# x1 transposed part by part without its norm, the norm applied one stage later, and the later modulation's tiles loaded by GpSimd's queue

## The chip, the cores and the metric

The kernel runs on one core of one Trainium2 chip. The metric is the device time of one execution in microseconds (us), and the median over the executions of one kernel is what two kernels are compared by. Inside a core, TensorE (PE in the profile) multiplies matrices, VectorE (DVE) and ScalarE (ACT) work on tiles elementwise, GpSimd (POOL) and SyncE (SP) mostly issue DMA transfers here. Each engine works through its own instructions in the order in which the program wrote them, and waits at an instruction until the data that it needs are there.

## The reference

One block of a hybrid network for 256 tokens of width 2048, in float32:

```python
cs = silu(c)
mod = cs @ ada_w + ada_b
sh1, sc1, g1, sh2, sc2, g2 = split(mod, 6)
h = rmsnorm(x, norm1_w) * (1 + sc1) + sh1
...                      # h @ w_in, gated delta net -> o_a, sparse attention -> o_b
y = sigmoid(m_a) * (o_a @ w_branch_gdn) + sigmoid(m_b) * (o_b @ w_branch_nsa)
x = x + g1 * (y @ w_out)
h2 = rmsnorm(x, norm2_w) * (1 + sc2) + sh2
x = x + g2 * peer(h2, peer_wq, ...)
return rmsnorm(x, final_norm_w)
```

The change is at the line `x = x + g1 * (y @ w_out)`, called x1 below, at the line `h2 = ...`, and at the loading of the part of `ada_w` from which g1, sh2 and sc2 are made.

## The kernel before

Weights come from HBM as float32. To multiply in a faster number format without losing accuracy, each weight piece of 128x512 is cut in two: ScalarE casts it (`whi<-raw`), VectorE takes the rest (`wlo<-raw,whi`), and TensorE does three products, hi*hi, lo*hi and hi*lo. A class `Stream` does this for all weights in order: SyncE's queue loads 512 KB tiles into 4 buffers `raw`, `advance` cuts as many pieces ahead as there are buffers (5 in the first stream, 4 in the second), and `get` hands out the next piece.

The stages that matter here, in order of time: the projections of h with the gated delta net as side work, attention, the two branch products (`wn`), then `y @ w_out` in four column blocks j = 0 to 3 of 512 columns (`wo`), then h2 and its first product with `peer_wq` (`wq`). Tokens stand in two blocks of 128, tb = 0 and 1.

**Side work.** Tasks written as Python generators are put in a list `bg`; between the groups of main matmuls a planner with its own rough cost model of every engine and of two DMA queues decides which task's next step is written into the program. So an edit that changes a modelled cost also changes the order in which later side work stands. One such side work is `ada_late`: 192 tiles `adas` of 128x512 (256 KB) with the columns of `ada_w` for g1, sh2 and sc2 are loaded into two buffers, and VectorE multiplies each with `crow` and sums it (`SCALAR_TENSOR_TENSOR adas<-adas,crow`). The load of a tile is written right behind the multiplication that frees its buffer. The same function runs again much later for g2, into tiles that the trace calls `ht`.

**wo, before.** For each block j, `x1_part` multiplies the sums in PSUM with g1 (`x<-ps,g1b`), adds x (`x<-x,xr`), lets ScalarE square the result and sum it into `ss1`, and stores it (`x1d`). In block 3 the last four row tiles are done for tb 0 first and then for tb 1, each followed by its part and by `x1_norm`, which makes r1 = 1/rms for the 128 tokens, and from it `dg`, a diagonal matrix.

**h2, before.** `h2_pairs` multiplies x1 with `dg` on TensorE: this transposes x1 and applies the norm at once, into PSUM. Three pairs stand ahead of the loop over the 16 row tiles k, the others in it. In the loop ScalarE makes the hi part from PSUM with scale and bias, VectorE makes the float32 value (`h32b`) from PSUM and subtracts, and TensorE does 12 matmuls of 256 columns with the wq piece of the row tile before.

All operations are recorded at one helper line, L294, so tiles tell them apart.

Of the kernel before, what the change touches and what calls it, by code (L numbers as in the profile page):

```python
# [160 lines left out]
def flat(ap, off, *dims):  # L161
    return bass.AP(tensor=ap.tensor, offset=ap.offset + off, ap=[list(x) for x in dims])
# [16 lines left out]
NO1 = 4  # L179
TKT = 2  # L180
GEND = 20.0
NPAIR = 3
ZPACE = 5.0
NGT = 3
NSET = 2
# [225 lines left out]
def _build(nc, tc, A, out, stacks, dump, at, stop_at):  # L411
# [300 lines left out]
        act(out, in_, AF.Sqrt, bias=epst, scale=scale)  # L712
        V.reciprocal(out, out)

    def ada_late(parts, crow, acol, row, room):

        raws = []
        n = 64 * len(parts)

        def load():  # L720
            m = len(raws)
            r = room(m)
            SP.dma_start(r, flat(A["ada_t"], (64 * (parts[m // 64] - 2) + m % 64) * 128 * 512, (512, 128), (1, 512)))
            raws.append(r)

        for _ in range(2):
            load()
        yield
        for i, part in enumerate(parts):
            for m in range(64):  # L730
                r = raws[64 * i + m]
                q = m % 4
                V.scalar_tensor_tensor(r, r, 1.0, crow(q), op0=OP.mult, op1=OP.mult,
                                       accum_out=acol[:, m // 4, q:q + 1])
                if len(raws) < n:
                    load()
                yield
            col = mcol[:, part, :]
            V.tensor_reduce(col, acol, axis=AX.X, op=OP.add)
            V.tensor_tensor(col, col, adabT[:, 16 * part:16 * part + 16], OP.add)  # L740
            if part == SC2:
                V.scalar_tensor_tensor(col, col, 1.0, n2T, op0=OP.add, op1=OP.mult)
            if part in (G1, G2):
                yield bg.now() + 4.0
                p = ps()
                PE.transpose(p[:16, 0:128], col, ident)
                S.copy(row, p[:16, 0:128])
                G.dma_start(flat(modr, D if part == G2 else 0, (128, 16), (1, 128)), row)
            done.add(part)
            yield  # L750

    ada_gen = ada_late((G1, SH2, SC2), lambda q: crow[:, 512 * q:512 * q + 512], sbp.tile([128, 16, 4], F32, name="acol"),
                       sbp.tile([16, 128], F32, name="adarow"),
                       lambda m: sbp.tile([128, 512], F32, name="adas", bufs=2))

    def ada_until(*parts):

# [277 lines left out]
    def kv_rot(a, o, dst, free):  # L1035

        rts = []
        for tb in range(2):
            r = rp.tile([128, 2, 128], F32, name="kv_t", bufs=3)
            S.copy(r, a[tb][:, o:o + 256].rearrange("p (g d) -> p g d", g=2))  # L1040
            rts.append(r)
        banks.give(free)
        yield from wait_for("rope")
        yield
        for tb in range(2):
            rope(rts[tb], rts[tb], tb, 2)
# [242 lines left out]
    def vcvs_task(a):  # L1289
        vt = []  # L1290
        for tb in range(2):
            r = rp.tile([128, 2, 128], F32, name="kv_t", bufs=3)
# [326 lines left out]

    st_1 = stack()  # L1620
    xp = pool(st_1, "xp", side=RIGHT)
    x1 = xp.tile([128, 2, D], F32, name="x1")
# [4 lines left out]
    dg = xp.tile([128, 2, 128], F32, name="dg")  # L1627

    def x1_part(tb, j, c, a, xr):
        w = WO[j][1]  # L1630
        V.tensor_tensor(x1[:, tb, c], a[:, :w], g1b[:, c], OP.mult)
        V.tensor_tensor(x1[:, tb, c], x1[:, tb, c], xr[:, tb, :w], OP.add)
        act(ps()[:, :w], x1[:, tb, c], AF.Square, accum_out=ss1[:, tb, j:j + 1])
        G.dma_start(x1d[tb, :, c], x1[:, tb, c])

    def x1_norm(tb):
        r = r1[:, tb:tb + 1]
        V.tensor_reduce(r, ss1[:, tb, :], axis=AX.X, op=OP.add)
        rsqrt(r, r, 1.0 / D)
        V.tensor_scalar(dg[:, tb, :], ident, r, None, op0=OP.mult)  # L1640

    def xr_load(j):
        o, w = WO[j]
        xr = xp.tile([128, 2, 512], F32, name="xr", bufs=2)
        G.dma_start(xr[:, :, :w], A["x"][:, :, o:o + w].rearrange("b p d -> p b d"))
        return xr

    xrs = [xr_load(0)]
    for j, (o, w) in enumerate(WO):
        c = slice(o, o + w)  # L1650
        xr = xrs[j]
        if j + 1 < len(WO):
            xrs.append(xr_load(j + 1))
        if j < len(WO) - 1:
            po = dense_all(f"wo{j}", oT(yh), oT(yl), 16, w) if j else po0
            for tb in range(2):
                x1_part(tb, j, c, po[tb], xr)
        else:
            act(r1, ss1[:, :, 0], AF.Sqrt)
            po = acc2()  # L1660
            dense(po, oT(yh), oT(yl), w, range(16 - NLAST), 0, 15)

            last = [stream.get() for _ in range(NLAST)]
            for tb in range(2):
                for i, (h, l) in enumerate(last):
                    k = 16 - NLAST + i
                    PE.matmul(po[tb][:, :w], oT(yh)(k, tb), h[:, :w], start=False, stop=False)
                    PE.matmul(po[tb][:, :w], oT(yh)(k, tb), l[:, :w], start=False, stop=False)
                    PE.matmul(po[tb][:, :w], oT(yl)(k, tb), h[:, :w], start=False, stop=k == 15)
                x1_part(tb, j, c, po[tb], xr)  # L1670
                x1_norm(tb)
        banks.give(2)
    ada_until(SH2, SC2)
    st_y.close()
    st_a.close()
    stream.close()
    dump("x1", x1)
    at("x1")


# [16 lines left out]
    def h2_pairs(k2s):  # L1697

        new = [ps() for _ in k2s]
        for tb in range(2):  # L1700
            for k2, p in zip(k2s, new):
                for i in range(2):
                    k = 2 * k2 + i
                    PE.matmul(p[:, i * 256 + tb * 128:i * 256 + tb * 128 + 128], x1[:, tb, k * 128:(k + 1) * 128],
                              dg[:, tb, :], start=True, stop=True)
        return new


    pairs = h2_pairs(range(NPAIR))
    q4 = [ps() for _ in range(4)]  # L1710
    for k in range(17):
        if k == 0:
            stream.advance(0)
        if k < 16:
            pk = pairs[k // 2][:, k % 2 * 256:k % 2 * 256 + 256]
            hi, lo, _ = h2_of(k)
            h32 = xp.tile([128, T], F32, name="h32b", bufs=2)
            act(hi, pk, AF.Identity, bias=mcol[:, 3, k:k + 1], scale=mcol[:, 4, k:k + 1])
            V.tensor_scalar(h32, pk, mcol[:, 4, k:k + 1], mcol[:, 3, k:k + 1], op0=OP.mult, op1=OP.add)
            V.tensor_tensor(lo, h32, hi, OP.subtract)  # L1720
            if k % 2 == 0 and len(pairs) < 8:
                pairs += h2_pairs([len(pairs)])
        if k:
            h, l = stream.get()
            hi, lo, _ = h2_of(k - 1)
            for ct in range(4):
                w, wl_ = h[:, ct * 128:(ct + 1) * 128], l[:, ct * 128:(ct + 1) * 128]
# [214 lines left out]
    def g2_task():  # L1942
# [4 lines left out]
        start = bg.now()  # L1947
        for m, v in enumerate(ada_late((G2,), lambda q: crow[q // 2][:, q % 2 * 512:q % 2 * 512 + 512],
                                       small[:, 0:64].rearrange("p (n q) -> p n q", q=4), small[0:16, 128:256],
                                       lambda m: room[:, m % 2 * 512:m % 2 * 512 + 512])):  # L1950
# [131 lines left out]
```

## Time and profile before

| | us |
|---|---|
| median of 3 executions | 2616.61 (2616.02 to 2620.22) |
| profiled execution, its time | 2617.43 |
| its span in the trace | 2615.3 |
| TensorE busy in the span | 2551.7 |
| VectorE busy | 1870.9 |
| ScalarE busy | 1416.9 |
| GpSimd busy | 520.5 |

The span is the time from the first to the last instruction in the trace; 2.1 us of the execution's time lie around it. TensorE is busy in 98% of the span, so the 64 us in which it is idle are spread over few places, and an edit tells in the time by the idle time and the work that it adds to TensorE or takes from it.

### The profile page before, as it was taken

To read this page: it belongs to the slowest core of one execution; us is meant where nothing else is said; L and a number is where in the kernel's file an instruction comes from. 1 tells how busy PE (TensorE), PEld (TensorE's weight loads), DVE (VectorE), ACT (ScalarE), POOL (GpSimd) and SP (SyncE) were. 2 spreads that over 40 slices of the span, in tenths; PEclk is the share of its full clock that TensorE was granted. 3 is DMA by queue.
4 is the path that set the end of the run, shared out by engine and by line. 5 is a ranking of instruction groups with operands and counts; after the bars stand their busy time and mean duration, and the time that the engine had idled before them with its cause. 6 is when DMAs were issued, how large, how long until landed. Compare 5 with 4: busy or idle time off the path is not lost.

```text
span 2615.3 us, 42819 instructions
## 1 busy us (share of the span) xinstructions
PE 2551.7 (98%) x14746; PEld 2121.7 (81%) x14746; DVE 1870.9 (72%) x4089; ACT 1416.9 (54%) x2907; POOL 520.5 (20%) x467
## 2 busy tenths in 40 slices
PE   7999999999999999999999999999999999999998
PEld 5777777687877877999998888888778888888886
DVE  5667777777778776889885555555588887766666
ACT  4445756556555444555555555555555555655555
POOL 0001000000000000016666666662011112000000
PEclk9999999999999999999999999999999999999999
DMA  8997866777676887456667776776698888555554
GB/s 326 333 334 267 278 222 221 236 238 268 209 252 227 293 291 265 173 181 183 178 186 186 186 189 186 189 186 199 215 308 293 289 289 292 190 189 186 190 187 153
DMA packets 229658, 605.65 MB, mean 232 GB/s; under 512 B 60032, under 2 KB 60496, under 8 KB 228800
## 3 DMA queue, kind: packets, MB, share of 16 engines
q1 hardware_dynamic: 168192, 537.29, 59.1%
q0 software_dynamic: 49728, 41.50, 9.1%
q10 hardware_dynamic: 11520, 24.12, 2.4%
q8 instruction: 116, 1.90, 0.3%
q14 instruction: 102, 0.84, 0.1%
HBM read 572.76 MB, written 30.04 MB: 230 GB/s over the span
## 4 chain that ended last, share of the span: by engine, by line
PE 84%; DVE 6%; DMA 4%; ACT 3%; issue 2%; ACTq 0%; SPq 0%; DVEq 0%; POOLq 0%
PE ps L294 84%; DVE wlo L294 2%; DMA adas<-ada_t 1%; DMA raw<-w_in 1%; ACT whi L294 1%; DMA ht<-ada_t 1%; DVE adas L294 1%; ACT L294 1%; DVE cv L294 0%; DMA big<-x 0%; DVE A L294 0%; ACT gsq L294 0%; ACT o L294 0%; DVE x L294 0%; DMA mix<-partd 0%
## 5 line engine op out<-in xcount | busy, mean ns | idle before, releaser
L294 DVE TENSOR_TENSOR wlo<-raw,whi 128x512 fp32r<-128x512 f32 (+2 forms) x1632 | 1097.8, 685 | 508.8 <-ACT whi L294 449.6
L294 ACT CAST whi<-raw 128x512 fp32r<-128x512 f32 (+2 forms) x1632 | 996.1, 617 | 756.6 <-PE ps L294 571.7
L294 PE MATMUL ps<-ht,whi 128*128 128x256 f32 (+1 forms) x3152 | 817.7, 335 | 0.8 <-DVE ht L294 0.8
L294 PE MATMUL ps<-ht,wlo 128*128 128x256 f32 x2304 | 648.6, 281 | 0.3
L294 PEld LDWEIGHTS ps<-ht,whi 128*128 128x128 f32 x3152 | 533.6, 188 | 68.7 <-DVE ht L294 1.0
L294 PE MATMUL ps<-whi,ht 128*128 128x512 f32 (+2 forms) x1536 | 519.0, 401 | 11.2 <-ACT whi L294 7.6
L1860 POOL DMA_INDIRECT gated<-gate,place x256 | 415.2, 1622 | 287.0 <-DMA gated<-gate,place 172.9
L294 PEld LDWEIGHTS ps<-ht,wlo 128*128 128x128 f32 x2304 | 434.2, 188 | 1.0 <-DVE wlo L294 0.7
L294 PE MATMUL ps<-wlo,wh 128*128 128x512 f32 x1024 | 406.4, 397 | 3.0 <-DVE wlo L294 3.0
L294 PE MATMUL ps<-whi,wl 128*128 128x512 f32 x1024 | 406.3, 397 | 0.0
L294 PE MATMUL ps<-whi,wh 128*128 128x512 f32 x1024 | 403.1, 394 | 2.0 <-ACT wh L294 2.0
L294 PEld LDWEIGHTS ps<-whi,ht 128*128 128x128 f32 x1536 | 289.8, 190 | 86.5 <-issue 10.7
L294 PE MATMUL ps<-wlo,ht 128*128 128x512 f32 (+2 forms) x768 | 301.1, 392 | 3.1 <-DVE wlo L294 3.0
L294 PEld LDWEIGHTS ps<-wlo,wh 128*128 128x128 f32 x1024 | 192.6, 188 | 51.8 <-DVE wlo L294 4.1
L294 PEld LDWEIGHTS ps<-whi,wh 128*128 128x128 f32 x1024 | 192.6, 188 | 50.2 <-ACT wh L294 2.3
L294 PEld LDWEIGHTS ps<-whi,wl 128*128 128x128 f32 x1024 | 192.6, 188 | 44.8 <-DVE wl L294 0.2
L294 ACT CAST wh<-A 128x256 fp32r<-128x256 f32 x256 | 103.9, 407 | 134.9 <-PE ps L294 128.7
L294 PEld LDWEIGHTS ps<-wlo,ht 128*128 128x128 f32 x768 | 146.5, 191 | 32.3 <-DVE wlo L294 7.7
L294 DVE SCALAR_TENSOR_TENSOR adas<-adas,crow 128x512 f32<-128x512 f32 x192 | 131.5, 685 | 40.0 <-DMA adas<-ada_t 39.5
L294 DVE TENSOR_TENSOR wl<-A,wh 128x256 fp32r<-128x256 f32 x256 | 108.7, 425 | 47.4 <-ACT wh L294 46.6
L294 POOL DMA_DIRECT2D gates<-gated x128 | 68.6, 540 | 358.5 <-DVE A L294 346.3
L294 ACT COPY aj<-ps 128x256 f32<-128x256 f32 x91 | 33.9, 373 | 78.9 <-PE ps L294 74.6
(322 smaller groups left out, 2198.6 us busy)
## 6 DMA issues: line engine op xcount, KB each, us to landing
raw<-u SPq DMA_DIRECT2D x256, 512.0 KB
raw<-v SPq DMA_DIRECT2D x256, 512.0 KB
raw<-w_in SPq DMA_DIRECT2D x170, 512.0 KB
adas<-ada_t SPq DMA_DIRECT2D x192, 256.0 KB
raw<-ada_w SPq DMA_DIRECT2D x64, 512.0 KB
gated<-zero ACTq DMA_DIRECT2D x64, 256.0 KB
raw<-wn SPq DMA_DIRECT2D x32, 512.0 KB
raw<-wo SPq DMA_DIRECT2D x32, 512.0 KB
```

The source lines that it names most:

```text
L294: r = f(*args, **kw)
L1860: nc.gpsimd.indirect_dma_start(gated[tb].rearrange("i j (t o) -> (i j t) o", o=1), bass.IndirectOffsetOnAxis(ap=place[:, tb, n:n + 1], axi ...
```

## The change

Four things change.

1. x1 is no longer kept. `x1_part` writes the sum into the tile `xr` that held x, and `x1_turn` transposes it on TensorE with the identity, into PSUM, from where ScalarE copies it to `x1T`. For blocks 0 to 2 the square and the transpose are side work (`x1_task`); ahead of block 3 the program waits, in writing, until all their steps are written. In block 3 they stand right behind each part.
2. The norm: instead of `dg`, `x1_norm` spreads r1 over all partitions by a matmul (`ps<-ccom,r`) and a copy to `r1b`.
3. The h2 loop: VectorE makes `h32b` = x1T * scale * r1b, ScalarE makes hi from `h32b` plus the bias, and VectorE makes lo from `h32b`, the bias and hi.
4. The tiles `adas` are loaded by GpSimd's queue; the loads for g2 stay with SyncE's. `kv_t` has 4 buffers for 3.

```diff
-    def ada_late(parts, crow, acol, row, room):
+    def ada_late(parts, crow, acol, row, room, queue):
...
-            SP.dma_start(r, flat(A["ada_t"], (64 * (parts[m // 64] - 2) + m % 64) * 128 * 512, (512, 128), (1, 512)))
+            queue.dma_start(r, flat(A["ada_t"], (64 * (parts[m // 64] - 2) + m % 64) * 128 * 512, (512, 128), (1, 512)))
...
-                       lambda m: sbp.tile([128, 512], F32, name="adas", bufs=2))
+                       lambda m: sbp.tile([128, 512], F32, name="adas", bufs=2), G)
...
     def x1_part(tb, j, c, a, xr):
-        w = WO[j][1]
-        V.tensor_tensor(x1[:, tb, c], a[:, :w], g1b[:, c], OP.mult)
-        V.tensor_tensor(x1[:, tb, c], x1[:, tb, c], xr[:, tb, :w], OP.add)
-        act(ps()[:, :w], x1[:, tb, c], AF.Square, accum_out=ss1[:, tb, j:j + 1])
-        G.dma_start(x1d[tb, :, c], x1[:, tb, c])
+        x = xr[:, tb]
+        V.tensor_tensor(a, a, g1b[:, c], OP.mult)
+        V.tensor_tensor(x, x, a, OP.add)
+        G.dma_start(x1d[tb, :, c], x)
+
+    def x1_square(tb, j, xr):
+        act(ps(), xr[:, tb], AF.Square, accum_out=ss1[:, tb, j:j + 1])
+
+    def x1_turn(tb, j, xr):
+        p = ps()
+        for i in range(4):
+            PE.transpose(p[:, i * 128:(i + 1) * 128], xr[:, tb, i * 128:(i + 1) * 128], ident)
+        S.copy(x1T[:, 4 * j:4 * j + 4, tb * 128:(tb + 1) * 128], p.rearrange("p (k t) -> p k t", k=4))
+
+    def x1_task(j, xr):
+
+        yield times.ready[xr.tensor.name] + LAG
+        for tb in range(2):
+            x1_square(tb, j, xr)
+            yield
+            x1_turn(tb, j, xr)
+            yield
+        x1_done.add(j)
 
     def x1_norm(tb):
         r = r1[:, tb:tb + 1]
         V.tensor_reduce(r, ss1[:, tb, :], axis=AX.X, op=OP.add)
         rsqrt(r, r, 1.0 / D)
-        V.tensor_scalar(dg[:, tb, :], ident, r, None, op0=OP.mult)
+        p = ps()
+        PE.matmul(p[:, 0:128], r.to_broadcast([128, 128]), ident, start=True, stop=True)
+        S.copy(r1b[:, tb, :], p[:, 0:128])
...
+            bg.add(x1_task(j, xr))
         else:
+            bg.until(lambda: len(x1_done) == j)
...
                 x1_part(tb, j, c, po[tb], xr)
+                x1_square(tb, j, xr)
+                x1_turn(tb, j, xr)
                 x1_norm(tb)
...
-            h32 = xp.tile([128, T], F32, name="h32b", bufs=2)
-            act(hi, pk, AF.Identity, bias=mcol[:, 3, k:k + 1], scale=mcol[:, 4, k:k + 1])
-            V.tensor_scalar(h32, pk, mcol[:, 4, k:k + 1], mcol[:, 3, k:k + 1], op0=OP.mult, op1=OP.add)
-            V.tensor_tensor(lo, h32, hi, OP.subtract)
-            if k % 2 == 0 and len(pairs) < 8:
-                pairs += h2_pairs([len(pairs)])
+            h32 = xp.tile([128, T], F32, name="h32b", bufs=3)
+            V.scalar_tensor_tensor(h32, x1T[:, k, :], mcol[:, 4, k:k + 1], r1b.rearrange("p b t -> p (b t)"),
+                                   op0=OP.mult, op1=OP.mult)
+            act(hi, h32, AF.Identity, bias=mcol[:, 3, k:k + 1])
+            V.scalar_tensor_tensor(lo, h32, mcol[:, 3, k:k + 1], hi, op0=OP.add, op1=OP.subtract)
```

On TensorE, at the end of block 3, the matmuls of tb 0, of tb 1 and the first of the h2 loop (`ps<-ht,...`) stood together, with `dg` matmuls ahead of the loop:

```order
L294 MATMUL ps<-wlo,yh 128x512
L294 MATMUL ps<-whi,yl 128x512
L294 MATMUL ps<-dg,x_10524 128x128 x16
L294 MATMUL ps<-ht,whi 128x256 x2
L294 MATMUL ps<-ht,wlo 128x256
```

Now, between the last matmul of tb 0 and the first of tb 1 (`ccom,xr` are the transposes, `ccom,r` is the matmul that spreads r1):

```order
L293 MATMUL ps<-whi,yl 128x512
L293 MATMUL ps<-ccom,xr 128x128 x4
L293 MATMUL ps<-ccom,r_10543 128x128
L293 MATMUL ps<-whi,yh 128x512
L293 MATMUL ps<-wlo,yh 128x512
```

The transposes of tb 0 and the matmul with its r1 stand ahead of tb 1's last 12 matmuls; the same two rows stand again between tb 1 and the h2 loop. At the boundary of blocks 2 and 3 eight transposes stand in one row, `MATMUL ps<-ccom,xr 128x128 x8`.

On VectorE, from tb 1's norm into the h2 loop, before:

```order
L294 TENSOR_REDUCE r_10528<-ss_10527 128x1
L294 RECIPROCAL r_10528<-r_10528 128x1
L294 TENSOR_SCALAR dg<-ccom,r_10528 128x128
L294 TENSOR_TENSOR wlo<-raw,whi 128x512 x4
L294 TENSOR_SCALAR h32b<-ps,mcol 128x256
L294 TENSOR_TENSOR ht<-h32b,ht 128x256
```

Now on ScalarE at the same place (`ht<-h32b` makes hi):

```order
L293 ACTIVATE r_10543<-r_10543,epst 128x1
L293 COPY r1b<-ps 128x128
L293 CAST whi<-raw 128x512 x4
L293 ACTIVATE ht<-h32b,mcol 128x256 x3
L293 CAST whi<-raw 128x512
L293 ACTIVATE ht<-h32b,mcol 128x256
```

What moved is what hi hangs on: before it was made from PSUM beside `h32b`, now it is made from `h32b`. On both engines the row tiles follow each other as before, from the fourth on with one weight piece between two of them.

On GpSimd's queue, from attention's end through block 1 of wo, there is now (sa, sb, g1b and xr are loads of the mix, of g1 and of x):

```order
L293 DMA adas<-ada_t 128x512 x8
L293 DMA sa<-mixd 128x1024
L293 DMA sb<-mixd 128x1024
L293 DMA adas<-ada_t 128x512 x20
L293 DMA g1b<-modr 128x2048
L293 DMA xr<-x 128x2x512 x2
L293 DMA x1d<-xr 128x512 x2
L293 DMA xr<-x 128x2x512
L293 DMA adas<-ada_t 128x512 x9
```

Before, the `adas` rows stood on SyncE's queue, one after nearly every weight load. In the stages of the projections and attention the side work of all engines stands in another order than before; from the end of the h2 loop on, the order is the same.

## Rows read from the trace of the kernel before

**Rows 1.** The page: the span, and each engine's busy time.

```profile
span 2615.3 us, 42819 instructions
PE 2551.7 (98%) x14746; PEld 2121.7 (81%) x14746; DVE 1870.9 (72%) x4089; ACT 1416.9 (54%) x2907; POOL 520.5 (20%) x467
```

**Rows 2.** Window: length; busy time of PE, PEld, DVE, ACT, POOL; granted clock; DMA.

```profile
212.00:612.00 400.00, 381.32 (x2785) 295.15 (x2783) 297.72 (x837) 248.21 (x587) 4.91 (x14) 0.98 0.73 246
```

**Rows 3.** The critical chain: start, duration, what (two DMA pieces).

```profile
591.20 5.29 DMA mix<-partd
...
954.34 7.83 DMA adas<-ada_t
```

**Rows 4.** Waits of TensorE, 212 to 612 us, then 840 to 1045: sum, times, longest.

```profile
PE ps L294 <- DVE wlo L294: 3.0, 9, 0.7
...
PE ps L294 <- DVE wlo L294: 3.5, 5, 1.3
```

**Rows 5.** The tile adas: what VectorE waited for before it (us, times).

```profile
  DMA adas<-ada_t: 39.5, 24
```

**Rows 6.** Timeline from tb 0's last sums to the h2 loop.

```profile
1042.21 0.69 DVE L294 TENSOR_TENSOR x<-ps,g1b 128x512 f32<-128x512 f32 x1 [2.85 <-PE ps L294]
...
1043.66 0.60 ACT L294 ACTIVATE ps<-x 128x512 f32<-128x512 f32 x1 [5.03 <-DVE x L294]
...
1044.93 0.16 DVE L294 RECIPROCAL r<-r 128x1 f32<-128x1 f32 x1 [0.36 <-ACT r L294]
...
1045.47 1.60 PE L294 MATMUL ps<-dg,x 128*128 128x128 f32 x12 [0.50 <-DVE dg L294]
...
1047.93 2.16 ACT L294 CAST whi<-raw 128x512 fp32r<-128x512 f32 x4
...
1050.85 0.36 PE L294 MATMUL ps<-ht,whi 128*128 128x256 f32 x1
...
1052.03 0.39 PE L294 MATMUL ps<-ht,whi 128*128 128x256 f32 x1 [0.82 <-DVE ht L294]
```

**Rows 7.** Groups by form over the whole span: busy, mean ns, idle before.

```profile
L294 ACT CAST whi<-raw 128x512 fp32r<-128x512 f32 x1600 | 982.5, 621 | 738.7 <-PE ps L294 562.6 <-DMA raw<-w_in 65.1 <-ACT whi L294 39.7
...
L294 ACT COPY PT<-ps 128x512 f32<-128x512 f32 x16 | 9.3, 590 | 2.9 <-PE ps L294 2.3
...
L294 ACT ACTIVATE ht<-xnT,mcol 128x256 fp32r<-128x256 f32 x16 | 8.9, 594 | 1.2 <-DVE mcol L294 1.2
...
L294 ACT CAST whi<-raw 128x256 fp32r<-128x256 f32 x16 | 6.3, 409 | 4.8 <-PE ps L294 4.7
...
L294 DVE TENSOR_TENSOR wlo<-raw,whi 128x512 fp32r<-128x512 f32 x1600 | 1083.4, 690 | 498.0 <-ACT whi L294 439.2 <-PE ps L294 24.9 <-issue 3.0
...
L294 DVE SCALAR_TENSOR_TENSOR oal<-ps,gnw,oah 128x256 fp32r<-128x256 f32 x8 | 3.8, 480 | 1.1 <-ACT oah L294 1.1
```

**Rows 8.** The tile h32b: durations in ns (min/median/max), first and last start.

```profile
L294 DVE TENSOR_SCALAR h32b<-ps,mcol x16: 536/539/544, 1051.0 to 1075.9; 128x256 f32<-128x256 f32 x16
```

**Rows 9.** Timeline of TensorE: the matmul after the loop's 192nd, and four transposes.

```profile
952.68 0.60 PE L294 MATMUL ps<-ccom,sb 128*128 128x128 f32 x4
953.04 0.48 PE L294 MATMUL ps<-whi,yh 128*128 128x512 f32 x1
...
1078.40 0.40 PE L294 MATMUL ps<-ht,whi 128*128 128x256 f32 x2
```

**Rows 10.** Timeline around the boundary of blocks 2 and 3.

```profile
1026.76 2.69 ACT L294 CAST whi<-raw 128x512 fp32r<-128x512 f32 x5
...
1027.41 0.50 PE L294 MATMUL ps<-whi,yh 128*128 128x512 f32 x1 [1.22 <-ACT whi L294]
```

**Rows 11.** Windows as in rows 2: ahead of a lower clock, in it, and behind wo.

```profile
406.60:410.00 3.40, 1.43 (x8) 0.88 (x7) 3.31 (x8) 2.73 (x9) 0.00 (x0) 1.00 0.65 213
410.10:413.40 3.30, 3.14 (x9) 2.57 (x10) 1.21 (x4) 2.83 (x7) 0.00 (x0) 0.50 0.84 305
...
1045.00:1048.40 3.40, 1.60 (x12) 1.42 (x12) 2.15 (x7) 1.40 (x4) 0.54 (x1) 1.00 0.28 108
```

More of the change, by code (lines that the diff above doesn't have):

```diff
@@ L181 @@
 GEND = 20.0
-NPAIR = 3
 ZPACE = 5.0
@@ L1038, in kv_rot @@
         for tb in range(2):
-            r = rp.tile([128, 2, 128], F32, name="kv_t", bufs=3)
+            r = rp.tile([128, 2, 128], F32, name="kv_t", bufs=4)
             S.copy(r, a[tb][:, o:o + 256].rearrange("p (g d) -> p g d", g=2))
@@ L1291, in vcvs_task @@
         for tb in range(2):
-            r = rp.tile([128, 2, 128], F32, name="kv_t", bufs=3)
+            r = rp.tile([128, 2, 128], F32, name="kv_t", bufs=4)
             S.copy(r, a[tb][:, 0:256].rearrange("p (g d) -> p g d", g=2))
@@ L1621, in _build @@
     xp = pool(st_1, "xp", side=RIGHT)
-    x1 = xp.tile([128, 2, D], F32, name="x1")
+    x1T = xp.tile([128, KT, T], F32, name="x1T")
     g1b = xp.tile([128, D], F32, name="g1b")
@@ L1626, in _build @@
     r1 = xp.tile([128, 2], F32, name="r1")
-    dg = xp.tile([128, 2, 128], F32, name="dg")
+    r1b = xp.tile([128, 2, 128], F32, name="r1b")
+    x1_done = set()
     def x1_part(tb, j, c, a, xr):
-        w = WO[j][1]
-        V.tensor_tensor(x1[:, tb, c], a[:, :w], g1b[:, c], OP.mult)
-        V.tensor_tensor(x1[:, tb, c], x1[:, tb, c], xr[:, tb, :w], OP.add)
-        act(ps()[:, :w], x1[:, tb, c], AF.Square, accum_out=ss1[:, tb, j:j + 1])
-        G.dma_start(x1d[tb, :, c], x1[:, tb, c])
+        x = xr[:, tb]
[17 more added lines that the diff above has]
+        x1_done.add(j)
     def x1_norm(tb):
@@ L1639, in x1_norm @@
         rsqrt(r, r, 1.0 / D)
-        V.tensor_scalar(dg[:, tb, :], ident, r, None, op0=OP.mult)
+        p = ps()
+        PE.matmul(p[:, 0:128], r.to_broadcast([128, 128]), ident, start=True, stop=True)
+        S.copy(r1b[:, tb, :], p[:, 0:128])
     def xr_load(j):
         o, w = WO[j]
-        xr = xp.tile([128, 2, 512], F32, name="xr", bufs=2)
+        xr = xp.tile([128, 2, 512], F32, name="xr", bufs=3)
         G.dma_start(xr[:, :, :w], A["x"][:, :, o:o + w].rearrange("b p d -> p b d"))
@@ L1676, in _build @@
     stream.close()
-    dump("x1", x1)
     at("x1")
@@ L1695, in h2_of @@
         return h2[k // 2][:, k % 2, 0], h2[k // 2][:, k % 2, 1], h2[k // 2][:, k % 2].rearrange("p n t -> p (n t)")
[L1697 to L1709, printed above, removed]
     q4 = [ps() for _ in range(4)]
@@ L1714, in _build @@
         if k < 16:
-            pk = pairs[k // 2][:, k % 2 * 256:k % 2 * 256 + 256]
             hi, lo, _ = h2_of(k)
-            h32 = xp.tile([128, T], F32, name="h32b", bufs=2)
-            act(hi, pk, AF.Identity, bias=mcol[:, 3, k:k + 1], scale=mcol[:, 4, k:k + 1])
-            V.tensor_scalar(h32, pk, mcol[:, 4, k:k + 1], mcol[:, 3, k:k + 1], op0=OP.mult, op1=OP.add)
-            V.tensor_tensor(lo, h32, hi, OP.subtract)
-            if k % 2 == 0 and len(pairs) < 8:
-                pairs += h2_pairs([len(pairs)])
+            h32 = xp.tile([128, T], F32, name="h32b", bufs=3)
[3 more added lines that the diff above has]
+            V.scalar_tensor_tensor(lo, h32, mcol[:, 3, k:k + 1], hi, op0=OP.add, op1=OP.subtract)
         if k:
@@ L1949, in g2_task @@
                                        small[:, 0:64].rearrange("p (n q) -> p n q", q=4), small[0:16, 128:256],
-                                       lambda m: room[:, m % 2 * 512:m % 2 * 512 + 512])):
+                                       lambda m: room[:, m % 2 * 512:m % 2 * 512 + 512], SP)):
             yield -max(start + G2PACE * m, bg.now() + 2.0, v or 0.0)
```

## The prediction

> **What bounds the kernel now.** I read the page first: TensorE is busy in 2551.7 of 2615.3 us [rows 1]. So an edit can gain only where TensorE idles or does work that can go, and it loses wherever TensorE newly waits. Next the windows, for the places of the idle time: in the stretch of the projections it is 400 - 381.3 = 18.7 us [rows 2], and that is the largest. Then the chain and the waits, for what the loads of `adas` cost. The chain holds a load of 7.83 us from issue to use [rows 3], and VectorE waits for such loads 39.5 us in 24 places [rows 5]. But VectorE's wait reaches TensorE only after the weight pieces cut ahead have been used up: TensorE waited for `wlo` 3.0 us in the first stretch and 3.5 us in the second [rows 4]. Last the timeline from the end of wo into the h2 loop, where the arithmetic changes.
>
> There TensorE does not wait at all between the two token blocks. Its last matmul ends at 1045.47 - 0.50 = 1044.97, and tb 0's chain of norm runs from 1042.21 beside tb 1's 12 matmuls [rows 6]. The first matmul of the h2 loop starts at 1050.85, it pauses once for 0.82, and the loop's 192nd is done where the next one starts, at 1078.40 [rows 6, 9]: 33.4 us from the end of wo. Row tiles follow each other on VectorE every (1075.9 - 1051.0) / 15 = 1.66 us [rows 8].
>
> **The change, part by part.**
>
> *Transposes of blocks 0 and 1.* Four groups of four. A group keeps the next matmul back by 953.04 - 952.68 = 0.36 us [rows 9], so 4 x 0.36 = +1.4. They are side work in a stage that TensorE bounds. The squares and the 0.59 us copies [rows 7] go to ScalarE between casts, where it has room; I cost them at nothing there.
>
> *Boundary of blocks 2 and 3.* Eight transposes stand ahead of block 3's first matmul, and TensorE takes instructions in order. Multiply and add take 1043.66 - 1042.21 = 1.45 us for one token block [rows 6], two need 2.9. The first can start some 0.7 before block 2 ends, since tb 1's last three matmuls follow tb 0's. So tb 1's transposes are done 2.9 - 0.7 + 0.4 = 2.6 us after the end. Today TensorE goes on at once, then runs out of pieces and waits 1.22, because the squares and a table load on ScalarE hold the casts back until 1026.76 [rows 10]; starting 2.6 later, it should not run out. Net +1.4; the bounds are 0.8 (the transposes alone) and 2.6.
>
> *tb 0 against tb 1 in block 3.* Transposes and the matmul with r1 of tb 0 now stand ahead of tb 1's 12 matmuls, and these wait behind them. Today r1 is there at 1044.93 + 0.16 = 1045.09 [rows 6]. Now a copy of 0.59 [rows 7] stands between square and root on ScalarE, some of it in a gap, so about 1045.5; with the matmul (two records of 1.60 / 12 = 0.13 us [rows 6]) tb 1 starts at about 1045.8 instead of 1042.2. That is +3.6, and the price is sure within half a microsecond, since the rows are the same operations.
>
> *From tb 1 into the loop.* Counted from the end of wo: multiply to reciprocal 1045.09 - 1042.21 = 2.9, the copy 0.45, the r1 matmul and its handoff 0.4, the copy to `r1b` 0.3, four casts 2.16 [rows 6] beginning just before that copy ends, and the last `wlo` (0.69 [rows 7]) behind them: the first `h32b` starts 7.0 us after the end of wo. Today these casts lie beside the dg matmuls.
>
> *The loop.* In front of a row tile's hi now stands its own `h32b`, and on VectorE lo waits for that hi. From the fourth tile on, one cast stands behind hi on ScalarE and one `wlo` behind lo on VectorE, ahead of the next `h32b`. So a tile goes round: `h32b`, hi, cast, `wlo`. The trace has no such `h32b`; nearest is the 128x256 operation with one scalar per partition, 0.48. hi lies between a bare cast of that size, 0.41, and the activation with two scalars, 0.59; I take 0.50. Cast 0.62, `wlo` 0.69 [rows 7]. End to end 2.29. ScalarE begins an instruction 0.11 before the end of the one before (four casts take 2.16, not 2.48 [rows 6, 7]); with the same on both engines and three handoffs of 0.03, 2.17. Bounds 2.07 and 2.29. The first three tiles have no cast between them: 0.48 + 0.50 + 0.48 = 1.46. The last `h32b` starts at 7.0 + 2 x 1.46 + 13 x 2.17 = 38.1; hi, lo and the last matmuls add 2.5: 40.6 us after the end of wo for 33.4. That is +7.2 for both steps, though the loop loses its dg matmuls. By its own work TensorE would need 1.4 us a tile: 27.55 us from 1050.85 to 1078.40 [rows 6, 9], less the pause of 0.82, less 32 dg records at 0.13 (half of them stand in the loop, by the order), over 192 is 0.117, times 12.
>
> *The clock.* Where TensorE was busy in 1.43 of 3.4 us, the next stretch was granted 0.50, the 1.2 GHz level; behind wo, with 1.60 busy, it stayed at 1.00 [rows 11]. The new waits of 3 and 8 us hold about 0.8 us of TensorE's work each, so I expect a fall at each. A stretch at half speed costs at most 1.7 us of work, and nothing where TensorE idles. I take +2, from 0 to 5.
>
> *Loads of adas by GpSimd's queue.* They no longer stand between weight loads on SyncE, each of which waits for a buffer. 512 KB by GpSimd's queue took 5.29 us, 256 KB by SyncE's 7.83 [rows 3]. Upper bound of the gain: all of TensorE's waits for `wlo` in the two stretches, 6.5 [rows 4]. From the other side: 8 of these loads now stand behind loads of sa and sb that wait for VectorE and TensorE, and VectorE's sum, with every `wlo` behind it, waits for them; that could cost as much again as it saves. I take -4, from -6.5 to +4. GpSimd's issues cost nothing: it is busy in 520 of 2615 us [rows 1], and before the h2 stage hardly at all [rows 2].
>
> A page speaks against this step: the Trainium skill, "SBUF — State Buffer", "SBUF: two separate sides", says that while VectorE runs a copy in its two-port mode, GpSimd cannot write the descriptors of its transfers, and they stand still. Transfers by GpSimd's queue beside a busy VectorE took 5.29 us here [rows 3], which does not show it, and most of VectorE's work there is the two-input `wlo`, not copies. By the rule the term would be a loss and not -4; it is the fourth case below.
>
> *The side work's order.* In the projections every engine's order is new. I see no sign of a direction; 0, with 6 to each side, a third of that stretch's idle 18.7 [rows 2].
>
> **Sum.** 1.4 + 1.4 + 3.6 + 7.2 + 2 - 4 = +11.6 against the profiled execution's 2617.4, which makes 2629.0. The median of the runs is 0.8 lower than that execution, so 2628.2.
>
> **The rivals.**
>
> *No change:* hi is ahead, and the loop runs at TensorE's pace. Then tiles take 1.4 and not 2.17, the loop ends at about 8 + 16 x 1.4 = 30.4 instead of 40.6, and the sum is +1.4: 2618. For it speaks that three row tiles stand ahead of the first cast, and that four pieces are cut; against it, that the round through both engines is written into both orders. It becomes "no change" once a tile takes under 1.69 us, where 13 tiles give back 6.3 and the sum is 5.2.
>
> *Faster:* the new order of side work removes the projections' idle time. The price is at most 18.7, plus what the clock gives back: half-speed stretches as the one of rows 11 cost up to 1.7 each. With three quarters of the idle and two such stretches, -17.4: 2611. It decides once the projections give back 16.8, so that +11.6 becomes less than -5.2. Against it: most of that idle is waits for the delta net's own chain, only 3.0 of it for `wlo` [rows 4].
>
> *Much slower:* GpSimd's queue holds the adas loads up, and VectorE waits more than 39.5 us. If each of the 24 late loads waits for one more VectorE operation of 0.69, VectorE waits 16.6 more; the waits reached TensorE with 6.5 of 39.5 [rows 4, 5], so -4 turns into about +3, and with the loads behind sa and sb into +4: 2636.
>
> **How the numbers follow.** A measurement of this kernel tells about 0.2%, 5.2 us, from no change. I give the forecast 0.70, no change 0.12, faster 0.10, much slower 0.08. Of the forecast's own spread (2617 to 2637: the clock from 0 to 5, adas from -6.5 to +4, the side work 6 to each side, seldom all at one end) one in twenty lies within 5.2. So slower 0.665 + 0.08, rounded 0.74; same 0.12 + 0.035, rounded 0.16; faster 0.10. The range that leaves out no more than two in ten is 2614 to 2637: below it lies most of the faster case, above it the worst of the fourth.
>
> **What would show it.** TensorE idle about 3 us before the first `ccom,r` matmul and again about 7 before the first `ht` matmul; `h32b` starts every 2.2 us instead of 1.66, with TensorE about two thirds busy; some 2 us of idle before the eight transposes; a granted clock of 0.5 once or twice from there on. VectorE's wait for adas well under 39.5. If `h32b` comes every 1.7 us, the loop's term is wrong; if the projections' idle differs by more than 6 us from 18.7, the side work's term is.

## The result, and the profile after

The changed kernel takes 2657.0 us (median of 4 executions, 2653.4 to 2660.0) where the kernel before takes 2616.3 beside it (2615.9 to 2620.2): 1.0153 times the time, 95% interval 1.0140 to 1.0166. The direction is the one predicted. The size is not: +40.7 us for +11.6, far above the range's upper end of 2637.

The page of the changed kernel, to be read against [rows 1]:

```profile
span 2654.8 us, 42820 instructions
PE 2562.4 (97%) x14718; PEld 2127.9 (80%) x14718; DVE 1871.9 (71%) x4087; ACT 1422.6 (54%) x2918; POOL 627.6 (24%) x659
```

TensorE is busy 10.7 us longer, though it has 28 records fewer, and the span has grown by 39.5. So most of the loss is idle time; the rest is work at a lower granted clock and the added transposes. The windows tell where. The stretches are wn, wo, from wo's last matmul to the h2 loop's first, and the loop; columns as in [rows 2]. First the kernel before:

```profile
842.90:948.50 105.60, 103.89 (x482) 83.64 (x481) 82.15 (x187) 48.84 (x95) 4.22 (x8) 1.00 0.78 275
948.50:1044.60 96.10, 91.59 (x393) 72.42 (x391) 66.47 (x133) 43.37 (x78) 7.29 (x12) 1.00 0.81 281
1044.60:1050.90 6.30, 4.28 (x35) 3.72 (x33) 4.69 (x11) 3.84 (x9) 0.54 (x1) 1.00 0.24 88
1050.90:1078.30 27.40, 26.58 (x226) 26.35 (x225) 23.86 (x48) 17.25 (x33) 0.54 (x1) 1.00 0.44 154
```

Then the changed kernel, and in the fifth row the stretch of [rows 2]:

```profile
841.70:964.40 122.70, 109.24 (x482) 87.59 (x481) 84.57 (x195) 49.31 (x98) 21.36 (x40) 0.94 0.70 244
964.40:1075.00 110.60, 98.83 (x423) 77.45 (x421) 64.36 (x122) 48.16 (x87) 15.88 (x28) 0.97 0.67 234
1075.00:1083.50 8.50, 1.49 (x8) 0.72 (x6) 4.62 (x10) 4.34 (x10) 0.54 (x1) 0.84 0.21 75
1083.50:1116.80 33.30, 30.70 (x191) 25.84 (x192) 23.95 (x46) 16.11 (x33) 0.54 (x1) 0.94 0.34 116
212.00:612.00 400.00, 378.96 (x2792) 296.78 (x2791) 302.35 (x845) 250.10 (x588) 45.89 (x91) 0.98 0.71 242
```

wn is 17.1 us longer, wo 14.5, the way into the loop 2.2, the loop 5.9: together 39.7, the whole loss. Up to wn nothing is lost: it begins 1.2 us earlier than before. wn holds the same 482 matmuls on both sides, and the change does not touch one of them. TensorE idles in it 122.7 - 109.2 = 13.5 us for 1.7, and is busy 5.4 longer because the granted clock fell to 0.94 on the mean.

What it waited for in wn, in the form of [rows 4] (us, times, longest):

```profile
PE ps L293 <- DVE wlo L293: 10.6, 3, 6.4
```

The tile `adas`, the row that answers to [rows 5]:

```profile
  DMA adas<-ada_t: 65.6, 44
```

VectorE now waits 65.6 us for `adas`, not under 39.5 as the prediction wanted. But little of the rise lies where the time is lost: from the start of wn to the end of wo it waits 29.4 us for `adas`, for 26.5 in the kernel before. And the 6.4 us have another origin. The timeline of GpSimd's queue in the changed kernel, then VectorE's and TensorE's rows at the same two places:

```profile
880.94 0.54 POOL L293 DMA_DIRECT2D adas<-ada_t  x1 [2.79 <-DVE adas L293]
...
881.99 0.53 POOL L293 DMA_DIRECT2D sb<-mixd  x1
...
986.42 0.53 POOL L293 DMA_DIRECT2D g1b<-modr  x1
...
888.48 0.69 DVE L293 TENSOR_TENSOR sb<-ps,sb 128x512 f32<-128x512 f32 x1 [7.23 <-DMA sb<-mixd]
993.85 0.70 DVE L293 TENSOR_TENSOR ps<-ps,g1b 128x512 f32<-128x512 f32 x1 [6.07 <-DMA g1b<-modr]
...
891.88 0.80 PE L293 MATMUL ps<-wlo,obh 128*128 128x512 f32 x1 [6.36 <-DVE wlo L293]
998.91 0.79 PE L293 MATMUL ps<-wlo,yh 128*128 128x512 f32 x1 [5.28 <-DVE wlo L293]
```

Between the first two rows stands the load of `sa` alone. `sb` is issued right behind a load of `adas` that had itself waited for VectorE, and VectorE then stands 7.23 us until `sb` has landed. Every `wlo` is queued behind that sum, the pieces cut ahead run out, and TensorE stands 6.36. The same happens 105 us later with `g1b`. In the kernel before, the same loads and sums:

```profile
867.77 0.53 POOL L294 DMA_DIRECT2D sb<-mixd  x1 [3.32 <-issue]
949.17 0.53 POOL L294 DMA_DIRECT2D g1b<-modr  x1 [40.45 <-PE ps L294]
880.22 0.68 DVE L294 TENSOR_TENSOR sb<-ps,sb 128x512 f32<-128x512 f32 x1
...
973.96 0.69 DVE L294 TENSOR_TENSOR x<-ps,g1b 128x512 f32<-128x512 f32 x1
```

There GpSimd's queue had nothing else to do. It had stood 40.45 us at the load of `g1b` until TensorE released it at the end of wn, and issued it at once, 24.8 us ahead of its use, and `sb` 12.5 ahead. So this queue, while it was empty, fetched ahead by itself. Filled with loads that VectorE paces, it issues each load only when VectorE has reached the place in the program where the load is written, and that is right before it is needed.

### The profile page after: what moved, and what is told of

It reads as the page before. It is cut to its first block, busy times and chain, and to the rows that moved or that the text cites. A ratio compares the mean times of both kernels' runs of the same rounds, so it can differ in the third digit from the quotient of the medians.

```text
span 2654.8 us, 42820 instructions
## 1 busy us (share of the span) xinstructions
PE 2562.4 (97%) x14718; PEld 2127.9 (80%) x14718; DVE 1871.9 (71%) x4087; ACT 1422.6 (54%) x2918; POOL 627.6 (24%) x659
## 4 chain that ended last, share of the span: by engine, by line
PE 72%; issue 13%; DVE 5%; DMA 4%; POOL 3%; ACT 2%; ACTq 0%; POOLq 0%; SPq 0%; DVEq 0%
PE ps L293 72%; DVE wlo L293 2%; POOL adas L293 2%; DMA raw<-w_in 1%; DVE A L293 1%; DMA adas<-ada_t 1%; ACT whi L293 1%; ACT L293 0%; DMA ht<-ada_t 0%; DMA mix<-partd 0%; DMA xr<-x 0%; DVE adas L293 0%; DMA big<-x 0%; DVE cv L293 0%; ACT ht L293 0%
## 5 line engine op out<-in xcount | busy, mean ns | idle before, releaser
L293 POOL DMA_DIRECT2D adas<-ada_t x192 | 103.1, 537 | 649.8 <-DVE adas L293 624.8
L293 DVE SCALAR_TENSOR_TENSOR adas<-adas,crow 128x512 f32<-128x512 f32 x192 | 131.5, 686 | 65.8 <-DMA adas<-ada_t 65.6
```

Of the source, the lines that this page charges most:

```text
L293: r = f(*args, **kw)
```

## The experiments

Times are medians; the ratio is that of the run's executions to those of the kernel before on the same chip (2613 to 2616 us), with its 95% interval. The runs stand on four chips (e1 to e4; e5 to e8; e9 to e12; e13), so a difference between two of them by their medians can be off by some 3 us; where that matters, the ratios are compared too. The changed kernel stands at 1.0153.

| run | us | ratio |
|---|---|---|
| e1 queue only | 2637.7 | 1.0083 (1.0061 to 1.0106) |
| e2 order only | 2644.5 | 1.0113 (1.0096 to 1.0130) |
| e3 queue and order | 2629.6 | 1.0053 (1.0036 to 1.0069) |
| e4 loop ahead | 2618.8 | 1.0015 (1.0004 to 1.0026) |
| e5 before, GpSimd's queue | 2640.8 | 1.0088 (1.0072 to 1.0105) |
| e6 adas alone in the queue | 2650.5 | 1.0125 (1.0108 to 1.0142) |
| e7 tb 0's work last | 2618.1 | 1.0007 (0.9998 to 1.0017) |
| e8 no wait ahead of block 3 | 2614.6 | 0.9989 (0.9973 to 1.0005) |
| e9 GpSimd's queue till wn | 2630.8 | 1.0052 (1.0028 to 1.0077) |
| e10 before, order only | 2619.3 | 1.0011 (1.0000 to 1.0022) |
| e11 one cast | 2611.2 | 0.9979 (0.9968 to 0.9990) |
| e12 joint norm | 2610.3 | 0.9975 (0.9964 to 0.9986) |
| e13 without 18 loads | 2637.3 | 1.0097 (1.0072 to 1.0121) |

### Queue and order apart (e1, e2, e3)

The queue of `adas` enters twice: the loads themselves, and the planner, which counts a load on GpSimd's queue otherwise and so writes the side work in another order. A wrapper tells the planner one queue and uses the other, which makes the four cells.

```diff
-  ..., lambda m: sbp.tile([128, 512], F32, name="adas", bufs=2), G)
+  ..., Timed(nc.sync, "G", times))      # e1: SyncE's queue, GpSimd's order
+  ..., Timed(nc.gpsimd, "Q", times))    # e2: GpSimd's queue, SyncE's order
+  ..., SP)                              # e3: SyncE's queue and order
```

> The changed kernel with the modulation loads put back on SyncE's queue, while the planner is still told that they cost what they cost on GpSimd's queue: TensorE, VectorE and ScalarE keep the changed kernel's order row for row. Theory Q (loads queue up in GpSimd's queue behind loads that wait, and these behind them): the wn stage falls from 122.7 us back to 105 to 108, the wo stage from 110.6 to about 102, all loads wait for less, and the time is 2657 - 17 - 8 = 2632 us (2627 to 2638). Rival O (the other order of the side work is the loss): no change, 2650 to 2660 us. Rival X (x1's new form costs more than the 15.6 us forecast for it): 2640 to 2650 us, with the wo stage still near 110.

> The opposite cell: the loads stay on GpSimd's queue, but the planner counts them as SyncE's, so that TensorE, VectorE and ScalarE have the order that the kernel with SyncE's queue has. Q: still slow, 2645 to 2670 us, with VectorE's waits for adas and for sb, g1b and xr in the wn and wo stages as in the changed kernel. O: about 2630 us.

> The changed kernel with the loads on SyncE's queue and planned so: what is left against the kernel before is x1's new form, two buffers more, and nothing of GpSimd's queue. Q: 2632 us (2626 to 2638), that is 15 us over the kernel before, of which 7 to 8 in the h2 loop, 3.6 in the last block of wo, 1.4 at the boundary ahead of it and 1.4 in the transposes. O: about the same here. X: 2640 to 2650 us. If x1's new form costs nothing: 2617 us.

With the loads on SyncE's queue and every compute engine's order unchanged (e1), 19 us are gone by the medians, 18 by the ratios; the other way round (e2) only 12.5 and 10.5. With both (e3) 27 and 26 are gone. Theory Q holds: at either order the queue costs 15 to 19 us. O is not nothing: at GpSimd's queue the order costs 10.5 to 12.5, at SyncE's 8, where the two intervals just overlap. It shows in e1's stages: wo takes 101.0 us, as expected, but wn 112.1 and not 105 to 108. e2 came out half a microsecond under the lower end of what Q gave it. X falls: what is left in e3 over the kernel before is 14 to 15 us (15.1 by the medians of its own chip, 13.9 by the ratio), and 15.6 was forecast for x1's new form. The window of e3's wo stage:

```profile
947.30:1049.00 101.70, 96.17 (x422) 76.62 (x421) 67.58 (x134) 48.15 (x87) 7.31 (x12) 0.98 0.77 266
```

wn takes 104.9 us, as in the kernel before. Of the changed kernel's 17.1 there, x1's form has nothing, and of the 14.5 in wo it has 5.6.

e2 says more than its time, since VectorE's waits there are sorted (us, times, longest; 840 to 1000 us):

```profile
DVE ps L293 <- DMA g1b<-modr: 8.6, 1, 8.6
DVE sb L293 <- DMA sb<-mixd: 7.5, 1, 7.5
```

For `adas` it waited 12.6 us there in 9 places, 3.7 at the longest, and 37.4 in the whole kernel, less than before the change; and yet the run takes 2644.5 us. Its long waits are these two, for `g1b` and `sb`.

### The queue on the kernel before (e5, e10)

```diff
-  lambda m: sbp.tile([128, 512], F32, name="adas", bufs=2))        # kernel before
+  lambda m: sbp.tile([128, 512], F32, name="adas", bufs=2), G)     # e5, and kv_t with 4 buffers
+  ..., Timed(nc.sync, "G", times))                                 # e10: the same order, SyncE's queue
```

> The kernel before with nothing but the loads of adas moved to GpSimd's queue (and the fourth kv_t buffer, which that order of loads needs). If the loss of this part is the loads of sb and g1b standing behind loads of adas that wait for VectorE, it is there without x1's new form too: VectorE waits some 7 us for sb and 6 to 9 for g1b, and the time is 15 to 23 us over the kernel before (2630 to 2638). If the queue and x1's new form only do harm together: 2612 to 2620. The term of the prediction (-4): 2612.

> The kernel before with the fourth kv_t buffer and the planner told that the loads of adas cost what they cost on GpSimd's queue, while they stay on SyncE's: TensorE, VectorE and ScalarE have the order of the run that moved them on the kernel before. If the order alone loses, whatever x1's form: 8 us over the kernel before, about 2624 us (2621 to 2628), with a wait for wlo of some 3 us in wn. If it lost only beside x1's new form: 2614 to 2619.

e5 loses 23 to 24 us, at the upper end of what was expected, without anything of x1's new form: VectorE waits 6.9 us for `sb` and 5.3 for `g1b`. e10, its order with SyncE's queue, loses 3, which its interval (from 1.0000) barely tells from nothing. So the queue does its harm on its own, and the order's part depends on what else is there; the 8 us of e1 are not a price of the order as such.

### Where in the queue (e6, e9, e13)

e6 takes the other loads out of GpSimd's queue and leaves `adas` there.

```diff
-        G.dma_start(sa, mixd[2 * j])          # sb, g1b and xr alike
+        Timed(nc.sync, "G", times).dma_start(sa, mixd[2 * j])
```

> The changed kernel with the loads of adas left on GpSimd's queue, and the loads of sa, sb, g1b and xr moved from there to SyncE's; the planner is told the old costs, so that TensorE, VectorE and ScalarE keep their order row for row. If those loads were late because they stood behind loads of adas: VectorE's waits for sb (7.2 us) and g1b (6.1) are gone, and the time falls by 13 to 17 us to 2640 to 2644. If GpSimd's queue is too slow for adas by itself: no change, 2652 to 2660. If the loads on SyncE's queue now hold the weights up: slower than 2660.

6.5 us instead of 13 to 17: none of the three. SyncE's queue and VectorE in e6 show why:

```profile
843.86 38.71 SPq L293 DMA_DIRECT2D raw<-wn  x9
...
883.43 0.36 SPq L293 DMA_DIRECT2D sb<-mixd  x1
...
889.61 0.69 DVE L293 TENSOR_TENSOR sb<-ps,sb 128x512 f32<-128x512 f32 x1 [7.41 <-DMA sb<-mixd]
```

Behind nine weight loads that each wait for a buffer, `sb` is as late as behind `adas`. The experiment moved the queueing instead of removing it.

e9 switches the queue in time.

```diff
+    class Till:
+        def dma_start(self, *args):
+            (Timed(nc.sync, "G", times) if late else G).dma_start(*args)
...
+    late.append(1)
     pn0 = dense_all("wn0", ...)
```

> The changed kernel with the loads of adas on GpSimd's queue until the first block of wn is written, and on SyncE's from there on; the planner counts them as GpSimd's throughout. If the queue does its harm in wn and wo alone, where loads that wait (sa, sb, g1b, xr, x1d) share it: the time of the run with the queue alone put back, 2638 us (2632 to 2643). If the queue loses in the projections too: in between, 2644 to 2652. If it wins there: under 2632.

2630.8, with executions from 2622.5 to 2641.0. That is 1.2 us under the bound between the first case and the third, which such a spread can't tell apart; the second case is out. So the harm is in wn and wo, and the 144 loads by GpSimd's queue ahead of them cost nothing that shows.

e13 puts the cause itself to the test: it takes away just the loads that stand ahead of `sa`, `sb`, `g1b` and `xr`.

```diff
+            if skip:                                   # during wn0, and during wo0
+                r = raws[m - 2]
+                times.note("G", "dma_start", (r, src), {})
+            else:
                 r = room(m)
                 queue.dma_start(r, src)
```

> The changed kernel without the 18 loads of adas that stand in GpSimd's queue right ahead of the first loads of sa and sb (11) and of g1b and xr (7): VectorE sums an earlier tile again in their place, so part of the modulation is not computed from its weights. Every other instruction keeps its place. If sb and g1b are late because loads of adas stand ahead of them: VectorE's waits for sb (7.2 us) and g1b (6.1) go, with TensorE's waits for wlo behind them (6.4 and 5.3) and half of the half-speed stretches that follow (some 5): 2657 - 14 = 2643 us (2638 to 2646). If the loss is on the other side, loads of adas late behind sa, sb and x1d: 2652 to 2657.

By the medians 19.7 us are gone, by the ratios 14.7, where 14 were expected, and the run stands where e1 stands (1.0097 and 1.0083). In the profiled execution, the fastest of the four, VectorE no longer waits for `sb` or `g1b` at all; wn takes 108.0 us and wo 102.8, both at a granted clock of 1.00. In these two stages TensorE waits 5.4 us for `wlo`, where the changed kernel has 17.5 and e1 5.9: the 12.1 that are gone are about the two waits of 6.36 and 5.28. Its loads of `sb` and `g1b`, for 881.99 and 986.42 in the changed kernel:

```profile
863.00 0.54 POOL L293 DMA_DIRECT2D sb<-mixd  x1 [3.31 <-issue]
...
947.46 0.54 POOL L293 DMA_DIRECT2D g1b<-modr  x1 [1.91 <-DMA raw<-wo]
```

The other 174 loads of `adas` are still in GpSimd's queue, and VectorE still waits 51.6 us for `adas` in 37 places; this costs no more than on SyncE's queue. In that queue it is the loads behind `adas` that cost time, not `adas`. e13 also moves 18 x 256 KB less, and what that alone is worth was not run; but e1 and e9, which load all 192 tiles, issue `sb` and `g1b` early as well, and there VectorE waits for neither.

### x1's new form, step by step (e4, e7, e8, e11, e12)

Each of these is built on the one before it, the first on e3.

```diff
+            h32 = h32s[k]                           # e4: scaled ahead
+            if k < 15:
+                h32s.append(scaled(k + 1))          # the former scalar_tensor_tensor
             act(hi, h32, AF.Identity, bias=mcol[:, 3, k:k + 1])
...
                 x1_part(tb, j, c, po[tb], xr)
+            for tb in range(2):                     # e7: behind both token blocks' matmuls
                 x1_square(tb, j, xr)
                 x1_turn(tb, j, xr)
                 x1_norm(tb)
...
-            bg.until(lambda: len(x1_done) == j)     # e8: ahead of the last NLAST pieces instead
...
-            stream.advance(0)
+            stream.advance(3)                       # e11: one piece cut ahead of the loop, not four
...
-                x1_norm(tb)
+            x1_norm()                               # e12: r1 of both token blocks in one chain
```

> The run with queue and order as before the change, and in the h2 loop VectorE scales row tile k+1 before it makes the low part of row tile k, so that ScalarE's high part no longer stands alone between two VectorE steps. If the 2.17 us of a row tile are the chain of four steps (0.48 + 0.51 + 0.48 + 0.69 us): a row tile falls to 1.65 to 1.75 us, which is VectorE's own 0.48 + 0.48 + 0.69 or TensorE's, and the time by 15 x 0.45 = 7 us against the run with queue and order as before (about 2625 us). Rival: the loop is held by the clock or by TensorE, then no change (2632 us).

In the changed kernel a row tile went round like this; first VectorE's rows, then ScalarE's:

```profile
1092.22 0.48 DVE L293 SCALAR_TENSOR_TENSOR h32b<-x1T,mcol,r1b 128x256 f32<-128x256 f32 x1
1093.27 0.48 DVE L293 SCALAR_TENSOR_TENSOR ht<-h32b,mcol,ht 128x256 fp32r<-128x256 f32 x1 [0.58 <-ACT ht L293]
1093.78 0.69 DVE L293 TENSOR_TENSOR wlo<-raw,whi 128x512 fp32r<-128x512 f32 x1
1094.39 0.48 DVE L293 SCALAR_TENSOR_TENSOR h32b<-x1T,mcol,r1b 128x256 f32<-128x256 f32 x1
1092.73 0.51 ACT L293 ACTIVATE ht<-h32b,mcol 128x256 fp32r<-128x256 f32 x1 [1.16 <-DVE h32b L293]
```

From `h32b` to `h32b` it is 2.17 us, with hi on ScalarE alone between the first two steps of VectorE. In e4 VectorE has no gap left:

```profile
1065.05 0.48 DVE L293 SCALAR_TENSOR_TENSOR h32b<-x1T,mcol,r1b 128x256 f32<-128x256 f32 x1
1065.45 0.48 DVE L293 SCALAR_TENSOR_TENSOR ht<-h32b,mcol,ht 128x256 fp32r<-128x256 f32 x1
1065.87 0.69 DVE L293 TENSOR_TENSOR wlo<-raw,whi 128x512 fp32r<-128x512 f32 x1
1066.48 0.48 DVE L293 SCALAR_TENSOR_TENSOR h32b<-x1T,mcol,r1b 128x256 f32<-128x256 f32 x1
```

1.43 us a tile there, less than VectorE's sum of durations, since neighbours overlap; over the loop's 16 tiles it is 1.61. The time fell by 10.9 for 7 expected; the windows give 33.4 to 25.8 in the loop and 8.5 to 7.0 ahead of it, where the first `h32b` no longer stands behind four `wlo`.

> The run with the loop ahead, and in the last block of wo the squares, transposes and r1 matmul of token block 0 written behind the 12 matmuls of token block 1. The prediction's term for them standing ahead is +3.6 us: then 2618.75 - 3.6 = 2615. Rival: token block 0's chain moves behind the end and token block 1's chain waits for it there, so that nothing is won: 2618 to 2620.

wo went from 101.5 to 97.7 us, 3.8 for the 3.6 expected, but the way into the loop from 7.0 to 8.6, and the medians are 0.6 apart, the ratios 2 us. The rival was partly right. ScalarE in e7:

```profile
1044.41 0.27 ACT L293 COPY r1b<-ps 128x128 f32<-128x128 f32 x1 [0.84 <-PE ps L293]
1044.57 0.61 ACT L293 ACTIVATE ps<-xr 128x512 f32<-128x512 f32 x1
```

tb 1's square stands behind tb 0's copy of `r1b`, and that waited for TensorE.

> The run before this one, and the transposes of block 2 no longer have to be done ahead of block 3: they run as side work in it. TensorE's idle time at the boundary (1.4 and 0.8 us) and the half speed that follows it (3.4 us at 0.50, up to 1.7 us lost) go: 2612 us (2611 to 2613.5), and the wo stage is 96 to 98 us, as in the kernel before plus the transposes. Rival: the cut pieces run out all the same, as in the kernel before at 1026 us, and the time stays at 2614 to 2615.

The time fell by 3.5 us. It lies in the rival's range only because e7, from which the forecast counted, had come out 3 us higher than expected; the stage tells the two apart: wo takes 94.1 us, 2.0 less than in the kernel before, although it holds the transposes, and no stretch of it is at half speed.

> The run without the wait ahead of block 3, and ahead of the first row tile's high part ScalarE makes one cast of the next weights in place of four. The four take 2.2 us in which TensorE waits: three of them moved behind gives 1.6 us if nothing else is late (2613.0 us); if the casts are wanted at once by the second row tile, 0 (2614.6).

> The run with one cast, and the norm's factors of both token blocks in one chain (one reduction, one root, one reciprocal, one copy), in place of two chains that wait in each other's way on ScalarE. Token block 1's square began 1.3 us late behind token block 0's copy of r1b: 1.0 to 1.3 us less than the run with one cast, about 2612 us, and against the kernel before 0.1 to 0.2% faster. If the two chains hide in each other: no difference.

e11 gave 3.4 us where at most 1.6 was expected; its executions spread from 2600 to 2619, so the excess is not explained. e12 against e11 shows no difference that these runs can tell. Against the kernel before, e12 is faster by 0.25%, and its interval does not reach 1. wn is as before, and from wo on its windows read:

```profile
945.60:1039.10 93.50, 93.08 (x416) 75.03 (x415) 67.03 (x132) 46.66 (x84) 7.30 (x12) 1.00 0.85 289
...
1045.40:1069.90 24.50, 23.91 (x191) 23.89 (x191) 23.24 (x49) 17.67 (x36) 0.54 (x1) 0.93 0.55 174
```

wo is 2.6 us shorter than before, the loop 2.9, the way between them the same 6.3. So x1's new form is worth 0.25%, once `adas` stays on SyncE's queue and the waits that it brought are written away. How much of this the same rearrangements would give the kernel before was not run.

## Why the prediction was wrong

**The step that failed** is *Loads of adas by GpSimd's queue*, -4 us with bounds of -6.5 and +4. On the kernel before it measures +23 to +24 (e5), and in the changed kernel 26 to 27 with the order that hangs on it (e3 against the changed kernel). It asked who stands ahead of `adas` in the queue, found 8 loads behind `sa` and `sb`, and gave them at most +4. Of that size they are: in wn, behind loads of `sb` that waited for TensorE, VectorE waits twice for `adas`, 5.31 and 6.17 us, and TensorE 1.22 and 3.04 us behind it. It did not ask who stands behind `adas`. The order rows ahead of the prediction answer that: 20 loads of `adas`, then `g1b` and `xr`. A load of `adas` waits for VectorE's sum two tiles earlier, and VectorE does these sums at the place where the program wrote them; so 20 such loads tie whatever stands behind them to the program's pace. "GpSimd's issues cost nothing: it is busy in 520 of 2615 us" was the misreading beneath it. The issues themselves did cost nothing; but a busy share does not show that an idle queue was what fetched `sb` 12.5 and `g1b` 24.8 us ahead.

The upper bound of the loss was wrong for a second reason. It scaled VectorE's wait for `adas` by the share that reached TensorE before, 6.5 of 39.5 [rows 4, 5], and there is no such share. In e13 VectorE waits 51.6 us and wn runs at a clock of 1.00; in e2 it waits 37.4, and the run takes 2644.5 us. What decides is how long VectorE makes no `wlo` at one place. Its rows at the wait for `sb`, then at the longest wait for `adas`, with TensorE's wait behind that:

```profile
880.56 0.69 DVE L293 TENSOR_TENSOR wlo<-raw,whi 128x512 fp32r<-128x512 f32 x1
...
891.14 1.29 DVE L293 TENSOR_TENSOR wlo<-raw,whi 128x512 fp32r<-128x512 f32 x2
...
921.08 0.69 DVE L293 TENSOR_TENSOR wlo<-raw,whi 128x512 fp32r<-128x512 f32 x1
...
928.54 0.69 DVE L293 SCALAR_TENSOR_TENSOR adas<-adas,crow 128x512 f32<-128x512 f32 x1 [6.17 <-DMA adas<-ada_t]
...
929.15 1.29 DVE L293 TENSOR_TENSOR wlo<-raw,whi 128x512 fp32r<-128x512 f32 x2
...
929.90 0.50 PE L293 MATMUL ps<-wlo,obh 128*128 128x512 f32 x1 [3.04 <-DVE wlo L293]
```

From the end of one `wlo` to the start of the next it is 9.9 us at `sb`, where four sums with `sb` stand behind the wait, and 7.4 at `adas`. TensorE stood 6.36 and 3.04 of them; the pieces cut ahead covered 3.5 and 4.3.

**The fourth rival**, *much slower*, named the right queue and the right direction and forecast 2636, by the wrong loads. The rule of the page beside it (the Trainium skill, "SBUF — State Buffer", "SBUF: two separate sides": GpSimd cannot write the descriptors of its transfers while VectorE runs a copy in its two-port mode) is not needed for the loss: in e13 174 loads of `adas` go by GpSimd's queue, and the time is that of SyncE's queue. That run is no test of the rule, though: VectorE's copies in wn and wo take 3.3 us there, all of them out of PSUM. Nor is the row that the prediction held against it, a transfer by GpSimd's queue "beside a busy VectorE": VectorE was busy in 1.29 of its 5.30 us.

**x1's new form** was costed at 13.6 us and 2 for the clock. Together that is 15.6, and e3 measures 14 to 15. By its steps: the transposes, the boundary and tb 0 ahead of tb 1 were 6.4; wo grew by 5.6 in e3. From tb 1 into the loop and the loop were 7.2; they grew by 2.2 + 6.0 = 8.2. Both growths hold what the clock took. A row tile was to take 2.17 us and takes 2.17. What TensorE waits for ahead of the `ccom,xr` and `ccom,r` matmuls and the first `ht` can be read beside what was to show it (2 us ahead of the eight transposes, 3 ahead of the first `ccom,r`, 7 ahead of the loop):

```profile
1045.65 0.66 PE L293 MATMUL ps<-ccom,xr 128*128 128x128 f32 x4 [1.36 <-DVE xr L293]
1047.08 0.63 PE L293 MATMUL ps<-ccom,xr 128*128 128x128 f32 x4 [0.77 <-DVE xr L293]
...
1068.82 0.66 PE L293 MATMUL ps<-ccom,xr 128*128 128x128 f32 x4 [1.51 <-DVE xr L293]
1070.63 0.77 PE L293 MATMUL ps<-ccom,r 128*128 128x128 f32 x2 [1.16 <-DVE r L293]
...
1083.50 1.10 PE L293 MATMUL ps<-ht,whi 128*128 128x256 f32 x2 [4.34 <-ACT ht L293]
```

They are 2.1, 2.7 and, with the two waits of tb 1's own transposes and r1 (1.51 and 1.16 again), 7.0. The boundary (+1.4, at most 2.6) was not measured by itself: taking it away gave 3.5 (e8), but that holds the half-speed stretch behind it, which the prediction counted under the clock, and a wait that the kernel before had too, since e8's wo is 2.0 shorter than there.

**The clock** (+2 for x1's form) fell where it was expected (means of 0.97, 0.84 and 0.94 in wo, on the way into the loop and in the loop), and besides in wn, behind the wait for `sb`, where 5.4 us of longer busy time went. **The side work's order** was to be 0 with 6 to each side: the stretch of the projections lost nothing (21.0 us idle for 18.7 in [rows 2], and wn begins earlier). Its part in the loss lies in wn, between 3 us (e10) and 10.5 to 12.5 (e2 against the changed kernel): with the loads on SyncE's queue, the changed kernel's order leaves 5.9 us of waits for `wlo` in wn and wo (e1), and the other order none (e3). Which of the moved steps does it stays open.

## What to carry to other kernels

Before a load goes into another queue, list what stands behind it there, and give each of those the time by which it now comes early; what comes early only because the queue is empty is lost as soon as something paced stands ahead of it. Price a wait by how long each single case keeps the next piece from being made, against what is cut ahead, and not by its sum. Where a value passes from one engine to another and back, write the next tile's first step ahead of this tile's last.

## What was not expected of the hardware

Issuing one of these loads took GpSimd 0.53 to 0.54 us and SyncE's queue 0.33 to 0.36, and neither shows in the time. What does is that the 512 KB of `sb` took 6.5 us from the start of the issue (881.99) until VectorE could use them (888.48) by GpSimd's queue, and 6.2 by SyncE's (883.43 to 889.61 in e6): in both kernels the load was issued later than that ahead of its use, and VectorE stood, whichever queue it was in.
